# Filter spectra finished in the convolution's rounds instead of stored and reloaded, with smaller array tiles in the filters' first and the convolution's last stage

## The chip, the cores and the metric

The kernel runs on one core of a Trainium2 chip. The metric is the device time of one execution in microseconds, as a median of several runs. TensorE multiplies matrices, VectorE (DVE), ScalarE (ACT) and GpSimd (POOL) work on vectors, SyncE (SP) issues most of the DMA transfers.

## The reference

One layer of an encoder on a sequence of 2048 positions and 1024 channels, in float32. Half of the mixed channels go through a long convolution (the "Hyena" group), half through a two-directional mLSTM; cross-attention into 256 memory tokens and a squared-ReLU MLP follow. The part that the change touches is this:

```python
hid = jnp.sin(fr1 * (z @ w1 + b1))          # z: position features, 2048 x 33
hid = jnp.sin(fr2 * (hid @ w2 + b2))
filt = (hid @ w3).reshape(L, 2, 2, 512)     # order, direction, channel
filt = filt * jnp.exp(-t * jnp.abs(deltas))[:, None, None, :]
two_sided = jnp.concatenate([filt[:, :, 0], zeros, jnp.flip(filt[1:, :, 1], axis=0)])
spec = jnp.fft.rfft(two_sided, axis=0)      # 4096 points

z, g1, g2 = u[..., :512], u[..., 512:1024], u[..., 1024:]
for o, gate in enumerate((g1, g2)):
    conv = irfft(rfft(z, n=2 * L, axis=1) * spec[:, o], n=2 * L, axis=1)[:, :L]
    z = gate * (conv + z * skip[o])
```

So two filters (orders 0 and 1) are made, brought to the frequency domain, and the sequence is convolved with the one, gated, convolved with the other and gated again.

## The kernel before

**Products.** The large projections are done with each operand split into a high and a low part, three products for one (`mm3`, L361 to L363, called R products or sweep products below). The transforms use plain float32 products; each of these leaves two matmul records in the trace.

**The transform.** The 4096-point transform is done in two stages as matrix products. The position is split into a slow part (row q, 128 of them) and a fast part j (16 of them). The first stage multiplies by the constant `f1` along the rows, for each j and 512 channels. Its output is stored to DRAM in an order by (frequency, j), and read back so that the second stage can multiply by one of 32 constant matrices `dm` along (frequency part, j). Going back, `em` undoes the second stage and `e2` the first.

**The filters** (`filters`). After two sine layers, eight steps (j2) make, for both orders and two values of j each, the forward and the backward filter (`beside`, L177 and L185, two products on halves of the rows at once), window them, and form sum and difference e[0], e[1]. `front` multiplies each by a 128x128 half of `f1` (L297, one full product each), copies the result (L298) and stores it to `fs0`, `fs1`. Then `blocks` reads them back, and 32 steps (2 orders x 16) multiply by `dm` (L344, two products a step), copy on ScalarE (L345) and store the finished spectrum to `hd` (L346).

**The convolution** (`hyena`). First, `spectrum(0, ...)` for eight j2: loads z from `hy` (L823), two row pairs (L177, L185), copies (L903), stores to `zs` (L906). Then, for each order o: 16 rounds, in each of which `load2` has fetched `dm`, `em`, the block of `zs` (L856) and the real and imaginary part of the filter from `hd` (L858, L859), `double` copies these to the other half of the partitions (L863 on ScalarE, L867 on VectorE), two products with `dm` (L926), the complex multiplication on ScalarE (L928, L929), VectorE (L930, L932) and GpSimd (L931), and, one step later (`late`), the product with `em` (`back`, L892), a copy (L893) and a store to `zg`. Then eight steps go back to time: order 0 with column pairs (`beside` with 64 columns each, L177 and L185) and, a step later, `spectrum(1, ...)`, the joined stage; order 1 with four full products a step (L949), the gate (L950), and the group norm that writes `yh`.

**What sets the order.** `weave` interleaves two generators by the costs that they yield: `filters` with the first eight column sweeps of the input projection (weights 230 and 200), then `hyena` with the remaining sweeps and the `natural` products (227 and 382). Within this, a list scheduler orders the instructions of each engine when the program is built, and each engine, and SP's DMA queue, works through its list in order. `beside` gives its first product a priority and makes the second wait for readers of two earlier banks, so that all are released together. PSUM has eight banks: four with tag `mm` for the projections and four with tag `hy` for the transforms. The convolution's large tiles share one ring of 10 buffers (tag `a`).

Of the kernel before, what the change touches and what calls it, by code (L numbers as in the profile page):

```python
# [18 lines left out]
L = 2048  # L19
# [8 lines left out]
def shape_constants():  # L28
# [15 lines left out]
    c_win = np.stack([win, winb], 0)  # L44
# [17 lines left out]
    f1h = np.zeros((2, 2, 32, 2, 64))  # L62
    e2h = np.zeros((2, 2, 2, 64, 128))
    for h in range(4):
        f1h[h // 2, h % 2, :, h % 2] = own
        e2h[0, h // 2, h % 2, :, 32 * h:32 * h + 32] = inv
        e2h[1, h // 2, h % 2, :, h::4] = inv
# [9 lines left out]
    for par in range(2):  # L77
# [12 lines left out]
    dm = dm.reshape(32, 128, 128)  # L90
# [7 lines left out]
        "c_f1": f1.transpose(1, 0, 2),  # L98
        "c_f1h": f1h.reshape(128, 128),
        "c_e2h": e2h.reshape(4, 128, 128).transpose(1, 0, 2),  # L100
# [34 lines left out]
class Prog:  # L135
# [37 lines left out]
    def beside(self, first, second):  # L173
        n = self.banks.index(first[0].tensor.name)
        n = self.banks.index(first[0].tensor.name)
        held = self.banks[max(0, n - 4):max(0, n - 2)] if first[0].tensor.name != second[0].tensor.name else []
        b = self.nc.tensor.matmul(*second, start=True, stop=True)  # L177
# [6 lines left out]
        with self.tc.high_priority(2000):  # L184
            self.tc.keep_in_program_order(self.nc.tensor.matmul(*first, start=True, stop=True))  # L185
# [45 lines left out]
    def filters(self):  # L231
        nc, tc, a = self.nc, self.tc, self.a
        sd = [self.dram(f"fs{o}", (2, 128, 16, CH)) for o in range(2)]
        hd = self.dram("hd", (2, 32, 128, CH))
        sb, ta, tb = self.fsb, self.ta, self.tb
        if True:
# [4 lines left out]
            f1 = sb.tile([128, 2, 128], F32, name="f1")  # L241
            nc.scalar.dma_start(out=f1, in_=a["c_f1"])

            def sine(dst, src, b, fr, first=False):
# [11 lines left out]
                nc.scalar.activation(dst, u if len(dst.shape) == 2 else u.rearrange("p (q j) -> p q j", j=16), AF.Sin)  # L256

            hid = sb.tile([128, 16, 128], F32, name="hid")
            for c in range(4):
# [10 lines left out]
                sine(hid[:, :, 32 * c:32 * c + 32].rearrange("p j q -> p q j"), p2, 2, 3)  # L270
# [23 lines left out]
            def front(e, st, jj, o, js):  # L294
                for p in range(2):
                    pp = self.hy()
                    nc.tensor.matmul(pp, f1[:, p], e[p], start=True, stop=True)  # L297
                    nc.scalar.copy(st[p][:, jj], pp)  # L298
                    if jj == 1:
                        nc.sync.dma_start(out=sd[o][p, :, js], in_=st[p])  # L300

            nxt = windows(0)
            for j2 in range(8):
                js = slice(2 * j2, 2 * j2 + 2)
                yield 14
# [17 lines left out]
            def blocks(o, i):  # L323
                p, k = divmod(2 * i, 16)
                dm = sb.tile([128, 2, 128], F32, tag="dm", name="dm", bufs=3)
                d = nc.sync.dma_start(out=dm, in_=a["c_dm"][:, 2 * i:2 * i + 2])
                if o == 0 and i < 3:
                    tc.keep_in_program_order(d)
                t = ta()
                nc.sync.dma_start(out=t, in_=sd[o][p, 8 * k:8 * k + 16].rearrange("(k r) j c -> (r j) k c", k=2))  # L330
                return dm, t

            order = [(o, i) for o in range(2) for i in range(16)]
            q = [blocks(*order[0]), blocks(*order[1])]
            for n, (o, i) in enumerate(order):
                if True:
                    yield 3.4
                    dm, t = q.pop(0)
                    if n + 2 < 32:
                        q.append(blocks(*order[n + 2]))  # L340
                    hs = ta()
                    for m in range(2):
                        pp = self.hy()
                        nc.tensor.matmul(pp, dm[:, m], t[:, m], start=True, stop=True)  # L344
                        nc.scalar.copy(hs[:, m], pp)  # L345
                    nc.sync.dma_start(out=hd[o, 2 * i:2 * i + 2].rearrange("k l c -> l k c"), in_=hs)  # L346
# [1571 lines left out]
```

## Time and profile before

| | |
|---|---|
| median of 3 runs | 3288.78 us (3285.28, 3288.78, 3291.98) |
| profiled execution | 3292.63 us, span from first to last instruction 3290.9 us |
| busy, of the span | PE 94%, DVE 60%, ACT 46%, POOL 38% |
| mean granted TensorE clock | 0.975 |
| DMA | 655.75 MB, mean 199 GB/s |

The trace names a line, an engine, an operation and its tiles (out<-in). "x" is a count. Matmul records overlap their neighbours, since products are pipelined; the distance of their starts is what a product takes of TensorE. PEld is the loading of the fixed operand. The stretches of time in the prediction are us from the first instruction.

### The profile page before, as it was taken

To read this page: it belongs to the slowest core of one execution; us is meant where nothing else is said; L and a number is where in the kernel's file an instruction comes from. 1 tells how busy PE (TensorE), PEld (TensorE's weight loads), DVE (VectorE), ACT (ScalarE), POOL (GpSimd) and SP (SyncE) were. 2 spreads that over 40 slices of the span, in tenths; PEclk is the share of its full clock that TensorE was granted. 3 is DMA by queue.
4 is the path that set the end of the run, shared out by engine and by line. 5 is a ranking of instruction groups with operands and counts; after the bars stand their busy time and mean duration, and the time that the engine had idled before them with its cause. 6 is when DMAs were issued, how large, how long until landed. Compare 5 with 4: busy or idle time off the path is not lost.

```text
span 3290.9 us, 45063 instructions
## 1 busy us (share of the span) xinstructions
PE 3097.7 (94%) x15113; PEld 2470.2 (75%) x15113; DVE 1971.7 (60%) x3316; ACT 1502.7 (46%) x2842; POOL 1242.2 (38%) x863
## 2 busy tenths in 40 slices
PE   7999999898999996799999998999999999999998
PEld 5656665674667885698988896888788887888876
DVE  7765224535556664676766556665755686565695
ACT  5533445643663343444444435545555543333335
POOL 0122000210222214534433106886756574434483
PEclk9999999999999997899999999999999999999999
DMA  5554998888787679758465526664644475444434
GB/s 188 187 201 148 313 307 257 261 240 249 215 246 231 200 250 309 210 164 262 140 223 196 195 78 225 207 219 160 218 156 157 157 234 166 132 140 140 130 96 163
DMA packets 473903, 655.75 MB, mean 199 GB/s; under 512 B 41278, under 2 KB 253374, under 8 KB 472648
## 3 DMA queue, kind: packets, MB, share of 16 engines
q1 hardware_dynamic: 437796, 594.30, 58.0%
q10 hardware_dynamic: 35876, 58.57, 5.2%
q8 instruction: 120, 1.97, 0.3%
q14 instruction: 111, 0.91, 0.1%
HBM read 437.73 MB, written 214.99 MB: 198 GB/s over the span
## 4 chain that ended last, share of the span: by engine, by line
PE 66%; DMA 14%; DVE 8%; issue 5%; ACT 3%; POOL 2%; SPq 1%; ACTq 0%; DVEq 0%; POOLq 0%
PE mm L361 14%; PE mm L363 13%; PE mm L362 13%; PE hy L363 5%; PE hy L361 5%; PE hy L362 5%; DVE wl L366 2%; PE hy L344 2%; DMA rw<-rows 2%; PE hy L297 2%; DMA wn<-in_w_in_dram 1%; DMA a<-zg 1%; DMA a<-hd 1%; PE hy L177 1%; PE hy L892 1%
## 5 line engine op out<-in xcount | busy, mean ns | idle before, releaser
L366 DVE TENSOR_TENSOR wl<-wn,wh 128x512 fp32r<-128x512 f32 (+1 forms) x364 | 285.9, 820 | 147.8 <-ACT wh L366 144.0
L1499 DVE TENSOR_TENSOR bl<-wr,bh 128x512 fp32r<-128x512 f32 x213 | 239.0, 1129 | 125.2 <-ACT bh L1498 125.1
L1498 ACT CAST ah<-w 128x512 fp32r<-128x512 f32 x284 | 176.5, 623 | 301.2 <-PE hy L362 153.4
L366 ACT CAST wh<-wn 128x512 fp32r<-128x512 f32 (+1 forms) x364 | 209.3, 619 | 211.6 <-DMA wn<-in_w_in_dram 57.9
L931 POOL TENSOR_TENSOR b<-b,a 128x512 f32<-128x512 f32 x64 | 88.6, 1384 | 574.4 <-ACT b L929 406.2
L361 PE MATMUL mm<-xh,wh 128*128 128x512 f32 x640 | 278.0, 436 | 12.3 <-ACT xh L366 5.5
L362 PE MATMUL mm<-xl,wh 128*128 128x512 f32 x640 | 270.2, 423 | 2.2 <-DVE xl L366 1.6
L363 PE MATMUL mm<-xh,wl 128*128 128x512 f32 x640 | 263.2, 411 | 0.0
L1499 DVE TENSOR_TENSOR al<-w,ah 128x512 fp32r<-128x512 f32 x236 | 226.0, 959 | 61.4 <-ACT ah L1498 61.1
L1498 ACT CAST bh<-wr 128x512 fp32r<-128x512 f32 x232 | 143.9, 622 | 231.9 <-PE mm L363 173.9
L363 PE MATMUL mm<-bh,al 128*128 128x512 f32 x576 | 225.4, 394 | 7.6 <-DVE al L1499 4.4
L361 PE MATMUL mm<-bh,ah 128*128 128x512 f32 x576 | 227.0, 394 | 0.9 <-DVE u L1624 0.8
L362 PE MATMUL mm<-bl,ah 128*128 128x512 f32 x576 | 226.1, 393 | 0.0
L361 PE MATMUL mm<-act,wh 128*128 128x512 f32 x512 | 200.4, 395 | 2.9 <-ACT wh L366 2.9
L362 PE MATMUL mm<-act,wh 128*128 128x512 f32 x512 | 200.8, 392 | 0.0
L363 PE MATMUL mm<-act,wl 128*128 128x512 f32 x512 | 199.6, 393 | 0.1
L1355 POOL TENSOR_TENSOR ssum<-ssum,sq 128x512 f32<-128x512 f32 x56 | 80.3, 1433 | 274.5 <-ACT sq L1354 274.5
L361 PEld LDWEIGHTS mm<-xh,wh 128*128 128x128 f32 x640 | 123.0, 192 | 71.8 <-issue 29.9
L361 PE MATMUL hy<-bh,ah 128*128 128x512 f32 x448 | 175.2, 391 | 0.0
L362 PE MATMUL hy<-bl,ah 128*128 128x512 f32 x448 | 174.6, 390 | 0.0
L363 PE MATMUL hy<-bh,al 128*128 128x512 f32 x448 | 174.4, 390 | 0.0
L362 PEld LDWEIGHTS mm<-xl,wh 128*128 128x128 f32 x640 | 122.7, 192 | 53.8 <-issue 26.2
(368 smaller groups left out, 8785.5 us busy)
## 6 DMA issues: line engine op xcount, KB each, us to landing
wr<-hc SPq DMA_DIRECT2D x224, 256.0 KB
w<-in_ff_w_dram SPq DMA_DIRECT2D x176, 256.0 KB
hc<-t SPq DMA_DIRECT2D x128, 256.0 KB
wn<-in_w_in_dram SPq DMA_DIRECT2D x100, 256.0 KB
hc<-q SPq DMA_DIRECT2D x96, 256.0 KB
fs<-a SPq DMA_DIRECT2D x32, 512.0 KB
a<-fs SPq DMA_DIRECT2D x32, 512.0 KB
hd<-a SPq DMA_DIRECT2D x32, 512.0 KB
```

The lines of the kernel that those rows point to most:

```text
L177: b = self.nc.tensor.matmul(*second, start=True, stop=True)
L297: nc.tensor.matmul(pp, f1[:, p], e[p], start=True, stop=True)
L344: nc.tensor.matmul(pp, dm[:, m], t[:, m], start=True, stop=True)
L361: mm(ps, lh, rh, start=start, stop=False)
L362: mm(ps, lh, rl, start=False, stop=False)
L363: mm(ps, ll, rh, start=False, stop=stop)
L366: both = (self.nc.scalar.copy(hi, src), self.nc.vector.tensor_tensor(lo, src, hi.bitcast(F32), ALU.subtract))
L892: nc.tensor.matmul(pg, em[:, m], y, start=True, stop=True)
L931: nc.gpsimd.tensor_tensor(xt, xt, hi[:, m], ALU.mult)
L1355: nc.gpsimd.tensor_tensor(ssum, ssum, sq, ALU.add)
L1498: self.nc.scalar.copy(hi, src)
L1499: eng.tensor_tensor(lo, src, hi.bitcast(F32), ALU.subtract)
```

## The change

- `filters` ends after `front`. The second stage (`blocks`, its 32 steps, the tensor `hd`) is gone.
- `hyena` loads the filter's first-stage output itself (`load_filter`: `dm` and two halves of a block of `fs`), two rounds ahead, and `response` makes the filter's spectrum one round ahead: two products with `dm` into `mm` banks, each evacuated by four copies of 64 partitions, two on ScalarE, two on VectorE. `double` is gone.
- `front` uses four products of 64 rows by 64 columns, for e[0], e[1] and two groups of 64 rows each, through a `beside` that takes any number of products. Each of its two banks receives one quarter from each row group.
- Rows are ordered as two groups of 64 by parity of q. With it, order 1's last stage becomes column pairs like order 0's, and constants and DMA patterns change: z, gates and `yh` move as two DMAs of 64 partitions, `zs` stores and `zg` loads as one of 128 partitions, `zs` loads and `zg` stores as two of 64.
- The yielded costs and the two weights of `weave` change.

```diff
-    def beside(self, first, second):
-        n = self.banks.index(first[0].tensor.name)
-        n = self.banks.index(first[0].tensor.name)
-        held = self.banks[max(0, n - 4):max(0, n - 2)] if first[0].tensor.name != second[0].tensor.name else []
-        b = self.nc.tensor.matmul(*second, start=True, stop=True)
+    def beside(self, *products):
+        names = [p[0].tensor.name for p in products]
+        n = min(self.banks.index(t) for t in names)
+        held = self.banks[max(0, n - 4):max(0, n - 2)] if len(set(names)) > 1 else []
+        b = self.nc.tensor.matmul(*products[-1], start=True, stop=True)
...
-            self.tc.keep_in_program_order(self.nc.tensor.matmul(*first, start=True, stop=True))
+            for p in reversed(products[:-1]):
+                self.tc.keep_in_program_order(self.nc.tensor.matmul(*p, start=True, stop=True))
...
             def front(e, st, jj, o, js):
+                pp = [self.hy() for p in range(2)]
+                self.beside(*((pp[p][64 * (p ^ g):64 * (p ^ g) + 64], f1[64 * g:64 * g + 64, 64 * p:64 * p + 64],
+                               e[p][64 * g:64 * g + 64]) for p in range(2) for g in range(2)))
                 for p in range(2):
-                    pp = self.hy()
-                    nc.tensor.matmul(pp, f1[:, p], e[p], start=True, stop=True)
-                    nc.scalar.copy(st[p][:, jj], pp)
+                    nc.scalar.copy(st[p][:, jj], pp[p])
...
-                yield 14
+                yield 9
...
-            def blocks(o, i):
-                p, k = divmod(2 * i, 16)
-                dm = sb.tile([128, 2, 128], F32, tag="dm", name="dm", bufs=3)
-                d = nc.sync.dma_start(out=dm, in_=a["c_dm"][:, 2 * i:2 * i + 2])
...
-                    for m in range(2):
-                        pp = self.hy()
-                        nc.tensor.matmul(pp, dm[:, m], t[:, m], start=True, stop=True)
-                        nc.scalar.copy(hs[:, m], pp)
-                    nc.sync.dma_start(out=hd[o, 2 * i:2 * i + 2].rearrange("k l c -> l k c"), in_=hs)
...
+        def load_filter(o, i):
+            dm = sb.tile([128, 2, 128], F32, tag="dm", name="dm", bufs=3)
+            nc.sync.dma_start(out=dm, in_=a["c_dm"][:, 2 * i:2 * i + 2])
+            p, k = divmod(2 * i, 16)
+            t = ta()
+            for g in range(2):
+                nc.sync.dma_start(out=t[own[g]], in_=of_block(fs[o][p, 64 * (p ^ g):64 * (p ^ g) + 64], k))
+            return dm, t
...
-            nc.sync.dma_start(out=hr[0:64], in_=src[0])
-            nc.sync.dma_start(out=hi[64:128], in_=src[1])
-            return dm, em, t, hr, hi
-
-        def double(i, hr, hi):
-            nc.scalar.copy(hr[64:128], hr[0:64])
...
-            nc.vector.tensor_copy(hi[0:64], hi[64:128])
+        def response(i, dm, t):
+            hr, hi = ta(), ta()
+            for m in range(2):
+                pp = self.mm()
+                nc.tensor.matmul(pp, dm[:, m], t[:, m], start=True, stop=True)
+                nc.scalar.copy(hr[0:64, m], pp[0:64])
+                nc.scalar.copy(hr[64:128, m], pp[0:64])
+                nc.vector.tensor_copy(hi[64:128, m], pp[64:128])
+                nc.vector.tensor_copy(hi[0:64, m], pp[64:128])
...
+            fq = [load_filter(o, i) for i in range(2)]
             nxt = load2(o, 0)
+            ready = response(0, *fq.pop(0))
             for i in range(16):
-                yield 3.5
-                dm, em, t, hr, hi = nxt
+                yield 4.6
+                dm, hr, hi = ready
+                em, t = nxt
+                if i < 14:
+                    fq.append(load_filter(o, i + 2))
                 if i < 15:
                     nxt = load2(o, i + 1)
+                    ready = response(i + 1, *fq.pop(0))
...
-                    if o == 0:
-                        own = [slice(64 * b, 64 * b + 64) for b in range(2)]
-                        self.beside(*((pp[own[b]], e2[:, b, own[b]], r[b][:, jj]) for b in range(2)))
-                    else:
-                        for p in range(2):
-                            nc.tensor.matmul(pp, e2[:, 2 + p], r[p][:, jj], start=p == 0, stop=p == 1)
+                    self.beside(*((pp[own[g]], e2, r[g][:, jj]) for g in range(2)))
...
-            weave(p.filters(), s, 230, 200)
+            weave(p.filters(), s, 80, 200)
...
-                      227, 382)
+                      271, 382)
```

118 lines of the change are left out of this document (47 added, 71 removed).

## The prediction

> **What bounds the kernel now.** I read the page first, then a table of time stretches, then the timeline at three places to get the true price of a matrix product, then the groups of the operations that the diff removes or adds, the DMA issues and the chain.
>
> ```profile
> PE 3097.7 (94%) x15113; PEld 2470.2 (75%) x15113; DVE 1971.7 (60%) x3316; ACT 1502.7 (46%) x2842; POOL 1242.2 (38%) x863
> DMA  5554998888787679758465526664644475444434
> ```
>
> TensorE is busy 94% of the span, VectorE 60%. The DMA digits say that slices 4 to 14 (330 to 1230 us) run their DMA engines at 70% or more. That is where the changed stages lie, so the stretches come next: filters' front (100 to 350), filters' second stage (350 to 480, the part that goes), and the convolution: first spectrum, rounds of order 0, the joined stage (order 0 back to time and spectrum of order 1), rounds of order 1, last stage.
>
> ```profile
> core 0: us, PE busy (x) PEld busy (x) DVE busy (x) ACT busy (x) POOL busy (x), PEclk, DMA share, GB/s
> 100.00:350.00 250.00, 240.66 (x920) 150.47 (x920) 158.72 (x254) 97.86 (x157) 56.24 (x32) 0.97 0.54 180
> 350.00:480.00 130.00, 130.00 (x473) 86.06 (x472) 26.41 (x40) 62.50 (x101) 0.00 (x0) 1.00 0.94 321
> 480.00:548.00 68.00, 62.96 (x254) 39.38 (x253) 26.66 (x39) 24.54 (x38) 0.00 (x0) 1.00 0.89 253
> 548.00:700.00 152.00, 138.41 (x727) 101.37 (x725) 76.63 (x122) 98.47 (x161) 41.97 (x32) 1.00 0.86 257
> 700.00:812.00 112.00, 96.52 (x487) 61.23 (x486) 46.32 (x70) 27.45 (x49) 0.00 (x0) 0.94 0.90 249
> 812.00:1004.00 192.00, 182.74 (x691) 127.11 (x689) 111.80 (x159) 123.74 (x187) 46.60 (x32) 0.96 0.76 221
> 1004.00:1130.00 126.00, 119.76 (x787) 101.47 (x786) 86.69 (x192) 38.52 (x77) 35.38 (x22) 0.97 0.81 247
> ```
>
> Between 350 and 480 us TensorE has no idle time at all, although DMA stands at 0.94 and 321 GB/s: that stage is bound by TensorE's work, and its traffic runs beside it. In the convolution TensorE idles 5.0, 13.6, 15.5, 9.3 and 6.2 us of the five stretches, lower bounds, because a record lasts beyond the start of the next. So the stretch from 100 to 1130 us is TensorE work plus some 50 us of stalls, and the change is worth what it takes from either. Bytes and copies are worth something only where they end a stall.
>
> A product's mean duration is no price, since products overlap. The pitch is.
>
> ```profile
> 392.19 0.39 PE L362 MATMUL mm<-xl,wh 128*128 128x512 f32 x1
> 392.42 1.02 PE L344 MATMUL hy<-a,dm 128*128 128x512 f32 x2
> 392.88 0.80 PE L363 MATMUL mm<-xh,wl 128*128 128x512 f32 x1
> 393.52 0.40 PE L361 MATMUL mm<-xh,wh 128*128 128x512 f32 x1
> ...
> 510.03 0.39 PE L361 MATMUL mm<-xh,wh 128*128 128x512 f32 x1
> 510.25 0.39 PE L362 MATMUL mm<-xl,wh 128*128 128x512 f32 x1
> 510.57 0.69 PE L177 MATMUL hy<-a,f 64*128 64x512 f32 x1
> ...
> 511.63 0.50 PE L363 MATMUL mm<-xh,wl 128*128 128x512 f32 x1
> 511.97 0.39 PE L361 MATMUL mm<-xh,wh 128*128 128x512 f32 x1
> ...
> 711.01 0.28 PE L362 MATMUL mm<-wl,xh 128*128 128x256 f32 x1
> 711.13 0.28 PE L363 MATMUL mm<-wh,xl 128*128 128x256 f32 x1
> 711.34 0.64 PE L177 MATMUL hy<-a,e 128*64 128x512 f32 x1
> 711.34 0.64 PE L185 MATMUL hy<-a,e 128*64 128x512 f32 x1
> ...
> 713.20 0.39 PE L361 MATMUL mm<-wh,xh 128*128 128x256 f32 x1
> 713.42 0.28 PE L362 MATMUL mm<-wl,xh 128*128 128x256 f32 x1
> ```
>
> First part: from 392.19 to 393.52 there are one full float32 product (two records) and two sweep products of 0.23 us pitch (510.03 to 510.25 shows the pitch): 1.33 - 0.46 = **0.87 us for a full product**. Second: from 510.25 to 511.97 one row pair (two products on halves of the rows) and two sweep products: 1.72 - 0.46 = **1.26 us for a lone row pair**, that is 0.87 for both halves at once and 0.39 for entering and leaving the split array. Third: from 711.13 to 713.42 two column pairs and two sweep products at 0.12: **2.05 us for two column pairs**, which is 2 x 0.87 and 0.3. L177 and L185 start at the same moment there, though both stream through all rows: column halves run side by side.
>
> The Trainium skill, "TensorE: Matmul & The Clock Gate", section "Measured speedup vs the span model", has a packed group last one product and about 4 ns for each further tile. By it the 32 groups of four below would cost 28 us and the front would give 27. The row of the lone pair shows 0.39 us more than one product, so I don't go by it.
>
> **The change part by part.**
>
> ```profile
> L297 PE MATMUL hy<-b,f 128*128 128x512 f32 x128 | 65.5, 624 | 0.0
> L949 PE MATMUL hy<-a,e 128*128 128x512 f32 x64 | 30.8, 624 | 2.8 <-DMA a<-zg 2.8
> L345 ACT COPY a<-hy 128x512 f32<-128x512 f32 x64 | 37.5, 587 | 62.1 <-PE hy L344 62.0
> L863 ACT COPY a<-a 64x1024 f32<-64x1024 f32 x32 | 33.5, 1046 | 73.6 <-DMA a<-hd 73.5
> L867 DVE COPY a<-a 64x1024 f32<-64x1024 f32 x32 | 22.1, 690 | 58.0 <-DMA a<-hd 50.0 <-DMA em<-in_c_em_dram 3.6 <-DMA kn<-st 2.8
> L903 DVE COPY a<-hy 128x512 f32<-128x512 f32 x32 | 21.6, 687 | 15.2 <-PE hy L185 9.8 <-DMA a<-hy 5.2
> L928 ACT ACTIVATE b<-hy 64x512 f32<-64x512 f32 x64 | 38.2, 596 | 8.2 <-PE hy L926 3.6 <-ACT a L893 1.9 <-DVE b L930 0.6
> ```
>
> *Filters' front on quarters.* 128 records of L297 are 64 full products: 64 x 0.87 = 55.7 us. They become 32 groups of four 64x64 products. No row shows four at once; row halves and column halves each do. Ends: 0.87 for a group (all four together) and 3.48 (one after another). I take 0.87 and 0.39 for the switch, because both kinds of pair behave so. In the changed program's order three of the 32 groups are parted by sweep products, so 35 passes: 35 x 1.26 = 44.1. **Saved: 11.6 us** (28 if switches cost nothing).
>
> *Last stage in column pairs.* 64 records of L949 are 32 full products, 27.8 us; now 8 times two column pairs, 8 x 2.05 = 16.4. **Saved: 11.4 us.** The third row block above is the operation itself, so this is the safest term.
>
> *Second filter stage, moved into the rounds.* L345 has 64 copies, one for each product: 64 x 0.87 = 55.7 us of TensorE work that stays, and moves from a stretch without idle time into the rounds. **0** on TensorE. Copies: ScalarE loses 37.5 + 33.5 and gains 128 half copies of 0.596 (L928's form), 76.3: +5 us in all, but +43 inside the rounds. VectorE loses 22.1 and gains 128 copies at 0.687 (L903 reads the same 512 columns of a bank), 87.9: +66 us, 2.1 us in each of 32 rounds. In the order-1 rounds VectorE would go from 111.8 of 192 us to about 145 of 220, 66%; ScalarE likewise to 66%. Neither becomes the bound; both queues get longer. The response of round i+1 stands ahead of round i's own products, so its copies have a round to finish, and they are queued ahead of the multiplications of L930 and L932 that `back` waits for.
>
> *DMA.* What goes is the store of hd and its two reloads, and the second read of dm.
>
> ```profile
> hd<-a SPq DMA_DIRECT2D x32, 512.0 KB
> a<-hd SPq DMA_DIRECT2D x64, 256.0 KB
> dm<-in_c_dm_dram SPq DMA_DIRECT2D x64, 128.0 KB
> a<-hy SPq DMA_DIRECT2D x64, 128.0 KB
> zs<-a SPq DMA_DIRECT2D x32, 256.0 KB
> zs<-a ACTq DMA_DIRECT2D x32, 256.0 KB
> ```
>
> That is 16.8 + 16.8 + 4.2 = 38 MB less; the reads of fs stay and take hd's place in a round, so a round's traffic is as now, while its TensorE work grows from four to six full products. DMA eases, most of it where it hid anyway.
>
> *What this does to the stalls.* Here the changed program's order decides. (a) Joined stage, now 15.5 us idle at a clock of 0.94 and DMA 0.90: in the new order 75 to 100 sweep products of 0.12 us stand between column pairs, 9 to 12 us, against 33 to 55 now. More cover for the same loads: -10 (ends -15 and 0). (b) Rounds, 13.6 + 9.3 idle now: counting products between L926's and its L892's place, the cover grows from 6 to 9 us to 7.5 to 12; against it stand the longer VectorE and ScalarE queues: -5 (ends -15 and +20, the latter if 0.6 us a round is waited for). (c) First spectrum stage, 5.0 idle now: its row pairs stand 17 sweep products apart today; in the new order 14 of the 16 stand back to back, with nothing between, and 24 sweep products follow after two responses before the first round. On SP's queue stand, each behind the other, z's loads, half of the stores to zs and the sweep's next weights. The pairs need 16 x 0.87 = 14 us. Until the last pair all eight loads must land (4.2 MB) and about four of the eight double stores (4.2 MB, since ten buffers hold 3.3 rounds), three loads earlier than the first pair: 6.8 MB at 0.29 MB/us between the rows' 253 and 321 GB/s is 24 us. So 10 us of idle time and some 3 at the handover, instead of 5: +8 (ends -5 and +36, below).
>
> Sum: -11.6 - 11.4 - 10 - 5 + 8 = **-30 us**. The profiled execution took 3292.63 us (span 3290.9), 3.9 above the median of 3288.78 and beside the slowest of the three runs; taken from the median, the forecast is **3259 us**, -0.9%.
>
> **The rivals.**
>
> *The first stage waits on its transfers (slower).* The same mechanism as (c) at its full price: all loads and stores of the stage, 12.6 MB, go through before TensorE proceeds, at 253 GB/s 50 us, with the landing of the last store behind it and the next load behind that.
>
> ```profile
> 498.21 4.84 DMA zs<-a
> ...
> 544.86 5.36 DMA a<-hd
> ```
>
> The second row stands for the load of the first block. 50 - 14 + 10 - 7 (two responses and 24 sweep products as cover) is 39 of idle time, +34. Where the transfers set the pace, (a) and (b) give nothing: -23 + 34 = +11, 3300 us. It decides from about 30 us of idle time in that stage on. For it: DMA at 0.89 in this stretch even when the pairs are spread, and stores among the longest steps of the chain. Against: half of the stores go out on ScalarE's queue, and nothing but the last rounds' buffers makes a load wait for a store.
>
> *The four quarters do not run together.* Two quarters on different rows write the same bank, on different partitions, and no row of the trace shows that; all row pairs here write two banks. If they take turns, a group costs 1.74 + 0.39: 32 x 2.13 = 68 against 55.7, +12 instead of -11.6, 3283 us. The Trainium skill, "TensorEngine Tiling (Array Packing)", section "Gotcha 1: PSUM Pressure", says that different row tiles cannot access one PSUM bank at the same time, which would give this. The column pairs, which share a bank across partitions and start together at 711.34, speak for the opposite.
>
> *The rounds' queues eat it.* (b) at its upper end: +25 against my sum, 3284 us. For it: 66% on two engines, with VectorE's L867 already behind DMA waits. Against: more cover in every round.
>
> *More is gained.* The lower ends of (a), (b), (c) with -23: 3231 us.
>
> **How the numbers follow.** Forecast 0.52; more gained 0.15; quarters in turn 0.08; queues 0.05; first stage 0.20. Of these the first two are faster by over 0.2% (6.6 us, about what a measurement of this kernel can tell), 0.67; the quarters and the queues lie at -5 to -6 us, within 0.2%, 0.13; the first stage is slower, 0.20. The forecast's own range is 3240 to 3277. The range to hold 8 in 10 runs from the upper part of "more gained", 3234, to just short of the full first stage, 3297.
>
> **What would show it.** In the new profile: quarter products starting within 0.2 us of each other in fours, next sweep product about 1.3 us later (else the second rival); last-stage column pairs at 2.05 us for two; the stretch from 100 us to the end of the last stage about 30 us shorter; the first spectrum stage with 10 to 15 us idle, the joined stage with 5; DMA bytes down by 38 MB. I am wrong if the first stage idles over 30 us, or if the rounds show TensorE waiting for L930's and L932's successors or for the copies of the response.

## The result and the profile after

| | before | after |
|---|---|---|
| median, us | 3288.79 (3285.28 to 3291.98, 4 runs) | 3241.74 (3236.51 to 3245.18, 4 runs) |
| ratio, 95% interval | 1 | 0.9854 [0.9836, 0.9872] |
| profiled execution; span, us | 3292.63; 3290.9 | 3245.18; 3243.5 |

The kernel became 47 us faster; 30 had been forecast. On the page of the profile after, TensorE's busy share is unchanged, VectorE has the extra copies, and the DMA moved 38 MB less than the 655.75 MB of before.

```profile
PE 3061.6 (94%) x15241; PEld 2442.3 (75%) x15241; DVE 2029.8 (63%) x3414; ACT 1499.1 (46%) x2871; POOL 1246.7 (38%) x863
PEclk9999899999999998999999999999999999999999
DMA packets 451633, 617.72 MB, mean 190 GB/s; under 512 B 39614, under 2 KB 247614, under 8 KB 450376
```

The table of stretches, cut at the new stage limits (front; first spectrum; rounds of order 0; joined; rounds of order 1; last stage), has the columns of the one in the prediction: time, its length, busy time of PE, PEld, DVE, ACT and POOL, granted clock, DMA share, GB/s.

```profile
100.00:371.00 271.00, 266.71 (x1244) 165.16 (x1242) 169.28 (x273) 107.39 (x177) 57.37 (x32) 1.00 0.54 172
371.00:421.00 50.00, 33.56 (x102) 15.27 (x102) 19.91 (x31) 15.96 (x28) 0.00 (x0) 0.76 0.99 316
421.00:624.00 203.00, 196.72 (x794) 134.31 (x794) 125.21 (x193) 135.80 (x225) 44.39 (x32) 0.98 0.73 203
624.00:753.00 129.00, 116.41 (x731) 85.68 (x731) 45.40 (x71) 32.71 (x64) 0.00 (x0) 0.93 0.77 242
753.00:964.00 211.00, 203.99 (x750) 135.87 (x750) 145.90 (x208) 140.71 (x228) 46.23 (x32) 1.00 0.72 197
964.00:1096.00 132.00, 118.95 (x799) 99.91 (x799) 93.38 (x206) 41.26 (x78) 42.04 (x28) 0.95 0.77 222
```

The second row is the new weak place: in the first spectrum stage 16 of 50 us are idle by records (the length of the stretch less TensorE's busy time), the DMA engines are full (0.99) and the granted clock is 0.76. The rounds (third and fifth row) are dense, with VectorE at 62% and 69%, and DMA at 0.73 and 0.72 where it stood at 0.86 and 0.76.

Busy time overstates work, since records overlap and grow longer at a low clock. So I also count each stage's *work* by pitch: number of products times 0.227 us (sweep, 512 columns), 0.120 (256 columns), 0.109 (transposition), 0.858 (full float32 product, or a pair or four of them side by side; full products back to back start at 421.55, 422.41, 423.27 and 424.12 us). What is left of the stage's length I call *idle*: waits, switches of the array and time lost to a low clock together. The front is counted from 100 us on; the stages run from the first product of one kind to the first of the next, the last one to the mLSTM's first transposition ("end"). "Filler" counts the narrow products (256 columns) ahead of that point. The other kernels of this table come below.

| length (idle), us | before | after | both_full | filler_back | before_filler | spread_first | spread_cover |
|---|---|---|---|---|---|---|---|
| front | 251.5 (29.3) | 271.1 (35.3) | 280.5 (19.1) | 270.2 (35.8) | 250.6 (29.3) | 269.5 (35.1) | 269.0 (35.5) |
| filters' second stage | 131.1 (2.1) | none | none | none | 131.3 (2.3) | none | none |
| first spectrum | 65.2 (11.2) | 50.4 (27.3) | 48.8 (23.9) | 50.5 (20.2) | 64.6 (10.6) | 65.7 (8.1) | 69.1 (6.1) |
| rounds, order 0 | 163.6 (17.0) | 202.4 (10.6) | 197.2 (6.4) | 218.9 (6.6) | 164.9 (18.3) | 202.8 (9.5) | 199.1 (11.3) |
| joined | 111.8 (34.5) | 129.5 (24.7) | 129.4 (24.5) | 124.0 (18.4) | 125.1 (25.4) | 109.9 (22.9) | 114.4 (16.9) |
| rounds, order 1 | 191.5 (19.1) | 210.5 (9.5) | 207.4 (6.4) | 220.9 (6.8) | 189.4 (16.5) | 197.4 (2.9) | 192.7 (9.1) |
| last | 126.3 (8.5) | 132.2 (23.8) | 135.8 (18.6) | 109.2 (14.1) | 128.7 (11.2) | 126.4 (25.0) | 120.7 (19.7) |
| end, us | 1140.9 | 1096.1 | 1099.0 | 1093.7 | 1154.5 | 1071.5 | 1065.1 |
| time behind the end | 2149.9 | 2147.4 | 2152.5 | 2145.0 | 2145.0 | 2154.6 | 2150.8 |
| filler | 1173 | 1051 | 1010 | 1288 | 1362 | 1089 | 1084 |

Of the 47.4 us that the span lost, 44.8 lie ahead of "end". The work ahead of it fell by 54.5 us: 27.5 for the front's quarters (64 to 32 passes of 0.858), 13.7 for the column pairs (32 to 16), and 14.6 because 122 filler products now come later, less 1.4 for six more sweep products. The idle time grew by 9.5; switches of the array, by the two prices that follow, add at most 16 to it (35 x 0.37 and 8 x 0.34), so the waits and the low clock fell by up to 6.

The timeline around a group of four in the front:

```profile
146.54 0.39 PE L337 MATMUL mm<-xl,wh 128*128 128x512 f32 x1
146.86 0.64 PE L175 MATMUL hy<-b,f 64*64 64x512 f32 x1
146.87 0.65 PE L184 MATMUL hy<-b,f 64*64 64x512 f32 x3
147.34 0.59 PE L175 MATMUL hy<-b,f 64*64 64x512 f32 x1
147.35 0.60 PE L184 MATMUL hy<-b,f 64*64 64x512 f32 x3
147.88 0.50 PE L338 MATMUL mm<-xh,wl 128*128 128x512 f32 x1
148.22 0.39 PE L336 MATMUL mm<-xh,wh 128*128 128x512 f32 x1
```

The four quarters start within 0.01 us of each other, twice (each product leaves two records). From 146.54 to 148.22 stand the group and two sweep products: 1.68 - 0.45 = 1.23 us for four quarters, 0.37 above one pass. In the last stage:

```profile
1003.74 0.29 PE L337 MATMUL mm<-wl,xh 128*128 128x272 f32 x1
1003.95 0.64 PE L175 MATMUL hy<-a,e 128*64 128x512 f32 x1
1003.96 0.64 PE L184 MATMUL hy<-a,e 128*64 128x512 f32 x1
...
1005.30 0.59 PE L184 MATMUL hy<-a,e 128*64 128x512 f32 x1
1005.82 0.39 PE L338 MATMUL mm<-wh,xl 128*128 128x272 f32 x1
1006.05 0.29 PE L336 MATMUL mm<-wh,xh 128*128 128x272 f32 x1
```

From 1003.74 to 1006.05 stand two column pairs and two products of 272 columns (0.127 us each): 2.31 - 0.25 = 2.06 us. Both prices are those of the prediction.

From the first spectrum stage and its handover to the rounds:

```profile
384.20 0.62 ACT L341 CAST wh<-wn 128x512 fp32r<-128x512 f32 x1 [4.49 <-DMA wn<-in_w_in_dram]
...
385.35 1.22 PE L175 MATMUL hy<-a,f 64*128 64x512 f32 x1 [4.07 <-ACT a L883]
...
398.28 0.66 PE L175 MATMUL hy<-a,f 64*128 64x512 f32 x1 [3.20 <-DMA a<-hy]
...
398.79 0.59 PE L175 MATMUL hy<-a,f 64*128 64x512 f32 x1
...
402.67 1.06 PE L175 MATMUL hy<-a,f 64*128 64x512 f32 x1
...
403.52 1.06 PE L175 MATMUL hy<-a,f 64*128 64x512 f32 x1
...
410.56 3.75 PE L840 MATMUL mm<-a,dm 128*128 128x512 f32 x4 [5.09 <-DMA a<-fs]
413.32 1.42 PE L336 MATMUL mm<-xh,wh 128*128 128x512 f32 x1
414.53 0.63 PE L337 MATMUL mm<-xl,wh 128*128 128x512 f32 x1
414.96 0.63 PE L338 MATMUL mm<-xh,wl 128*128 128x512 f32 x1
```

The pairs wait twice for ScalarE's copies (L883; 2.6 and 4.1 us; ahead of the second ScalarE itself had waited 4.5 us for the sweep's next weights), later for z's loads (3.2 us), and then the first response (L840) waits for the filter's load, which stands behind z's loads and the stores on SP's queue. Between the waits the products themselves are slow: the distance of two records is 0.85 us at 402.67 and 0.51 at 398.28, and the sweep products at 414.53 come every 0.43 us instead of 0.23.

The waits that fell on TensorE between 345 and 1150 us, the four largest of after (instruction, releaser, us in total, times, longest):

```profile
PE mm L840 <- DMA a<-fs: 17.9, 3, 9.0
PE hy L175 <- ACT a L883: 8.4, 3, 4.1
PE hy L175 <- DMA a<-zg: 5.4, 2, 4.0
PE mm L739 <- DVE cv L706: 3.9, 1, 3.9
```

and the largest of before in the same stretch:

```profile
PE hy L892 <- DVE b L932: 9.5, 9, 2.3
```

Before, the largest was `back` waiting, nine times, in the middle of the rounds for the complex multiplication. After, that wait is no longer among the large ones. Two of the three waits for a<-fs are at the handovers, for an order's first filter block (5.1 us at 410.56 and 9.0 at 743.17); the third, 3.8 us at 581.09, is inside order 0's rounds. The other rows are single waits in the first spectrum, joined and last stage.

### The profile page after: what moved, and what is told of

Read it like the earlier page. It is cut to its first block, busy times and chain, and to the rows that moved or that the text cites. A ratio compares the mean times of both kernels' runs of the same rounds, so it can differ in the third digit from the quotient of the medians.

```text
span 3243.5 us, 45260 instructions
## 1 busy us (share of the span) xinstructions
PE 3061.6 (94%) x15241; PEld 2442.3 (75%) x15241; DVE 2029.8 (63%) x3414; ACT 1499.1 (46%) x2871; POOL 1246.7 (38%) x863
## 4 chain that ended last, share of the span: by engine, by line
PE 74%; DMA 12%; DVE 7%; issue 3%; ACT 2%; POOL 1%; SPq 1%; ACTq 0%; DVEq 0%; POOLq 0%
PE mm L336 16%; PE mm L337 15%; PE mm L338 15%; PE hy L338 5%; PE hy L336 5%; PE hy L337 5%; PE hy L175 3%; PE mm L840 2%; PE hy L910 2%; PE hy L871 2%; DVE wl L341 1%; DVE bl L1479 1%; DMA wn<-in_w_out_dram 1%; DMA wn<-in_xa_wo_dram 1%; DMA rw<-rows 1%
## 5 line engine op out<-in xcount | busy, mean ns | idle before, releaser
L341 ACT CAST wh<-wn 128x512 fp32r<-128x512 f32 (+1 forms) x364 | 208.4, 617 | 196.3 <-PE mm L337 50.5
L337 PE MATMUL mm<-xl,wh 128*128 128x512 f32 x640 | 260.2, 407 | 2.2 <-DVE xl L341 1.6
L319 POOL TENSOR_TENSOR b<-b 128x512 f32<-128x512 f32 x32 | 57.4, 1793 | 295.4 <-DVE b L314 133.6
```

The source lines that it names most:

```text
L337: mm(ps, lh, rl, start=False, stop=False)
L341: both = (self.nc.scalar.copy(hi, src), self.nc.vector.tensor_tensor(lo, src, hi.bitcast(F32), ALU.subtract))
```

## The experiments

The question was which part carried the gain, and why the moved second stage might be worth more than the -7 us that the prediction's stall terms gave it (-10 - 5 + 8). Ratios are to the kernel before on the same chip, five rounds each, with 95% intervals. Listings are cut to the edit.

**The parts undone one by one.** *front_full*: the changed kernel with full products in the front.

```diff
-                pp = [self.hy() for p in range(2)]
-                self.beside(*((pp[p][64 * (p ^ g):64 * (p ^ g) + 64], f1[64 * g:64 * g + 64, 64 * p:64 * p + 64],
-                               e[p][64 * g:64 * g + 64]) for p in range(2) for g in range(2)))
...
+                    nc.tensor.matmul(pp, f1w[:, p], e[p], start=True, stop=True)
```

> The changed kernel with the filters' front on two full products again (the quarters put into a 128x128 constant with zeros elsewhere). Theory (product pitch): 64 full products at 0.87 us against 32 groups of four at 1.23 us in the new trace, so about +16 us, 3258 us, all of it between 100 us and the first spectrum pair. Rival (the front is paced by VectorE and GpSimd, not by TensorE): no change, 3242 us. Rival (the front's end moves, but the first spectrum stage, which waits for its transfers, takes the loss up): +5 us or less.

Measured: 3252.62 us, 0.9883 [0.9863, 0.9904], so about +9.5 us against the changed kernel (the two intervals overlap), between the expected 16 and the rivals. Its front lasted 279.8 us instead of 271.1: 27.5 us of work came back, 11 sweep products fewer stand there, and idle time, the switches of the array among it, fell from 35.3 to 19.0.

*last_full*: the changed kernel with two full products a value of j in order 1's last stage.

```diff
-                    self.beside(*((pp[own[g]], e2, r[g][:, jj]) for g in range(2)))
...
+                        for g in range(2):
+                            nc.tensor.matmul(pp, e2w[:, g], r[g][:, jj], start=g == 0, stop=g == 1)
```

> The changed kernel with order 1's last stage on four full products a step again (two accumulated, the constant filled up with zeros). Theory (product pitch): 32 full products at 0.87 against 8 times 2.05 us, +11 us, 3253 us. Rival: the last stage idles in the new trace for transfers and for VectorE (gaps of 4.2, 4.1 and 2.4 us), so the longer products fill gaps: +4 us or less.

Measured: 3246.31 us, 0.986 [0.984, 0.9881]: +2 us against the changed kernel, not to be told from nothing. 13.7 us of work came back, idle time in that stage fell from 23.8 to 16.4, and the convolution ended at 1090.8, 5 us *earlier* than with column pairs (41 filler products fewer, 4.9 us, stand ahead of its end).

*both_full*: both edits, so that only the moved second stage (with the row order, the yielded costs and the weights) is left of the change.

> Both of the above: what is left of the change is the filters' second stage moved into the rounds, with its DMA traffic gone. If the terms add, +27 us, 3269 us, and moving the stage alone is worth 20 us against the kernel before. If the whole gain came from the smaller array tiles, 3289 us. If the moved stage carries nearly all of it, under 3255 us.

Measured: 3256.18 us, 0.989 [0.987, 0.991]. Undoing both costs 12 us and not 27; what is left, the moved stage in its new order, is worth 36 us. Its rounds:

```profile
429.30:626.50 197.20, 192.37 (x784) 131.64 (x782) 123.76 (x192) 133.50 (x221) 44.38 (x32) 1.00 0.74 207
755.90:963.30 207.40, 203.23 (x748) 135.78 (x746) 145.17 (x207) 140.31 (x227) 45.85 (x32) 1.00 0.72 196
```

TensorE stands idle 4.8 and 4.2 us in them by its records, where before it was 13.6 and 9.3. With the table: idle time of rounds and joined stage falls from 17.0 + 34.5 + 19.1 = 70.6 to 6.4 + 24.5 + 6.4 = 37.3. That is 33.3 us of gain, and it is not the whole account. The front's idle time fell by 10.2 as well (716 sweep products stand in it for 551; granted clock 1.00 for 0.97); the first spectrum stage (with the second stage's 2.1 before) and the last stage idle 10.6 and 10.1 us more; and 163 filler products (19.6 us) slid behind the convolution, where the time grew by 2.6. Together the convolution ends 41.9 us earlier. Is it the bytes, the copies, or the TensorE work inside the rounds that ends the waits, and did the sliding of the filler matter?

**The bytes.** *more_traffic*: the changed kernel, and every round also stores its finished spectrum to a spare tensor that nobody reads.

```diff
+            nc.sync.dma_start(out=spare[0, i], in_=hr)
+            nc.sync.dma_start(out=spare[1, i], in_=hi)
```

> The changed kernel with the removed DMA traffic put back without its use: each round also stores hr and hi (512 KB each) to a scratch tensor, 33.5 MB in all, as much as the store of hd and its reloads were. Theory A (the moved stage gains because TensorE finds more of its own work between a round's products, bytes do not matter): within 5 us of the changed kernel, 0.9854 +- 0.002 of the kernel before. Theory B (the rounds stalled less because DMA was relieved by 38 MB): most of the 35 us that the moved stage is worth goes, ratio 0.993 or more.

Measured: 3239.53 us, 0.9841 [0.9821, 0.986], no slower than without. The DMA moved 651.29 MB. So the bytes saved are not the cause of the gain.

**Work in the rounds, without the change.** *idle_products*: the kernel before with two more products with `dm` in each round, whose output is not read.

```diff
+                    nc.tensor.matmul(self.mm(), dm[:, m], t[:, m], start=True, stop=True)
+                for m in range(2):
```

> The kernel before with two more full products in each round of the convolution, on the round's own dm and t into an mm bank that nobody reads: 64 products, 55.7 us of TensorE work by the pitch, and no change of DMA, copies or stages. Their result is not used. Theory A (cover): they fill stalls of the rounds (17.0 and 19.1 us idle there now, 10.6 and 9.5 in the changed kernel), and some 15 to 20 us of the sweep products move behind the convolution's end, where the mLSTM's first part leaves TensorE idle; so about +20 us, ratio 1.006. Theory B (DMA relief, TensorE is the bound): +50 us or more, ratio 1.015 or more.

Measured: 3348.8 us, 1.0188 [1.0174, 1.0202], far above Theory A's 1.006 and within Theory B's bracket (1.015 or more). The rounds by themselves did as Theory A has it: their idle time fell from 36.1 to 18.1 us with no byte and no copy less. But the interleaving changed ahead of them: the row pairs of the first spectrum stage came to stand back to back there too, and the handovers opened.

```profile
474.00:525.00 51.00, 27.38 (x69) 10.96 (x70) 11.07 (x16) 10.44 (x18) 0.00 (x0) 0.67 0.93 275
```

```profile
PE mm L925 <- DMA a<-zs: 21.2, 2, 10.8
PE hy L177 <- DMA a<-hy: 12.7, 2, 10.8
```

So this run mixed two things. *order1_products* puts the products into order 1's rounds alone (`for m in range(2 * o)`), which leaves the order of the stages ahead of them as it was.

> The kernel before, with two more products with dm in each of order 1's rounds and nothing else; their outputs are not read, so the result is the same. It puts the moved stage's TensorE work (16 x 2 x 0.87 = 27.9 us) into one set of rounds without touching the order of the stages ahead of them, which the version with products in both orders did. No bytes go. 159 of the narrow filler products slide behind the convolution (19.1 us), as there. Theory A (a round's own chain of loads, copies and multiplications sets its pace, and TensorE work that stands in it fills the wait): TensorE's idle time in order 1's rounds falls from 19.1 us to 6 to 8, the convolution ends at 1140.9 + 27.9 - 12 - 19 = 1138 us, and the whole takes 0 to +10 us against the kernel before, ratio 1.000 to 1.003. Rival (the idle time goes only because fewer bytes and no copies from hd are waited for): idle time stays at 17 to 19 us, the end at 1150 us, the whole +10 to +20, ratio 1.003 to 1.006.

Measured: 3311.31 us, 1.0061 [1.0043, 1.0079].

```profile
824.00:1022.00 198.00, 193.87 (x700) 127.24 (x698) 102.36 (x148) 115.41 (x175) 42.98 (x32) 0.99 0.68 197
```

```profile
PE mm L925 <- DMA a<-zs: 11.1, 1, 11.1
```

The idle time in order 1's rounds fell from 19.1 to 7.6 us, as Theory A said: they took 6.1 us longer (197.6 against 191.5) for 27.9 us of added work, of which 11.5 filled waits and some 10 stand in the place of filler or ahead of the rounds. The total went with the rival, for other reasons than the rival's: the filler that had covered the handover slid away and a wait of 11.1 us opened there (joined stage, idle 34.5 to 44.3), and the time behind the convolution grew by 11.8 us. Both theories missed those two.

**More cover by order alone.** *later_back*: the kernel before with `back` run two steps later instead of one, with two more `b` buffers and one more for `em`.

```diff
-                    late(lambda m=m, em=em, y=y, gs=gs, dst=by_block(gd, i): back(m, em, y, gs, dst))
+                    late(lambda m=m, em=em, y=y, gs=gs, dst=by_block(gd, i): back(m, em, y, gs, dst), 2)
```

> The kernel before with `back` (the product with em) two steps behind its round's product instead of one, and buffers for it (b 7, em 3). It adds cover between the two products, 1 to 1.5 us in the order built from it, and takes no work and no bytes away. Theory A (rounds stall on the chain from dm's product to em's): 10 to 20 us faster, ratio 0.995. Theory B: no change, ratio 1.000 +- 0.002.

Measured: 3273.4 us, 0.9958 [0.9945, 0.997]. The total came out at Theory A's size, but not by its mechanism: idle time in the rounds was 22.9 + 17.7 = 40.6 us and did not fall. But 41 us of other TensorE work, 21.6 of it filler, left the rounds in this order, so it is no clean test of cover; the waits of `back` for L932 still came to 8.0 us (9.5 before). The joined stage's idle time fell from 34.5 to 22.4, and 19 us of filler slid behind the end, where the time grew by 7.

**The filler.** It slid in nearly every kernel that was faster, so it could have been the gain. *filler_back*: the changed kernel with one weight of `weave` lowered.

```diff
-                      271, 382)
+                      240, 382)
```

> The changed kernel with one weight of the interleaving, 240 for 271, so that 1288 instead of 1051 of the narrow filler products stand before the mLSTM's first transposition: 237 x 0.12 = 28.4 us of TensorE work back into the convolution. Theory A (work behind the convolution is nearly free, since the mLSTM's first part leaves TensorE idle; so what counts is when the convolution ends): the convolution ends 15 to 28 us later, by what of the work does not fill a wait (30 sweep products now stand among the first row pairs too, and take 3 to 7 us of idle time there), the time behind it shortens by no more than 5 us, and the whole takes +12 to +22 us against the changed kernel, ratio to the kernel before 0.989 to 0.992. Rival (total TensorE work sets the time, wherever it stands): the time behind the convolution shortens by as much as the convolution grows, whole 0 to -7 us against the changed kernel, ratio 0.983 to 0.9855.

Measured: 3242.02 us, 0.9852 [0.9835, 0.987]. 28.4 us of TensorE work put back cost nothing, and the convolution still ended at 1093.7 us. Theory A's bracket (+12 to +22) is wrong. The rival's total fits, but not its mechanism: the time behind the end shrank by only 2.4 us. The work went into idle time: 131.2 us in all before, 101.9 now. Three stretches of it (first spectrum, joined, last):

```profile
370.00:421.00 51.00, 38.35 (x143) 20.19 (x142) 21.61 (x35) 18.22 (x32) 0.00 (x0) 0.87 0.97 320
640.00:764.00 124.00, 115.88 (x633) 80.25 (x630) 59.46 (x91) 39.87 (x69) 0.00 (x0) 0.97 0.84 265
985.00:1094.00 109.00, 100.83 (x746) 86.49 (x742) 78.39 (x181) 33.07 (x70) 39.64 (x28) 1.00 0.90 262
```

The granted clock is 0.87, 0.97 and 1.00 where the changed kernel had 0.76, 0.93 and 0.95. Length times missing clock gives at most 12 + 9 + 7 = 28 us lost there after, and 7 + 4 + 0 = 11 here: by these bounds up to 17 of the 29 us of idle time that went may be clock that was kept up.

*before_filler*: the same done to the kernel before (210 for 227).

> The kernel before with one weight of the interleaving, 210 for 227: 1362 instead of 1173 narrow filler products stand ahead of the mLSTM's first transposition, 189 x 0.12 = 22.7 us of TensorE work into the convolution. In the changed kernel 28.4 us of the same filler cost nothing (ratio 0.9852 against 0.9854; the convolution even ended 2.4 us earlier), because its stages wait for their own loads, stores and copies. Theory A (the same holds before the change: the convolution's own chain sets its end, and filler falls into waits): the convolution ends 0 to 6 us later, the whole -4 to +4 us, ratio 0.999 to 1.001. Rival (before the change TensorE's work counts, and the change made it stop counting by moving the second filter stage into the rounds): the convolution ends 15 to 23 us later, the time behind it shortens by 2 to 8 us, the whole +10 to +18 us, ratio 1.003 to 1.0055.

Measured: 3304.45 us, 1.0048 [1.0035, 1.0062], as the rival had it. The end came 13.6 us later (the rival said 15 to 23) for 22.7 us of work; the joined stage took all of it, and gave 9 us of idle time for it:

```profile
711.00:836.00 125.00, 112.56 (x537) 74.61 (x536) 60.12 (x91) 36.65 (x61) 0.00 (x0) 0.97 0.88 241
```

So in the kernel before, added TensorE work shows up in the time, and in the changed kernel it doesn't, as these two weights place it. The sliding of 122 products is not what the changed kernel gained by: with 115 more of them than the kernel before had, it is as fast.

**The handovers.** *spread_first*: the changed kernel with twice the yield in the first spectrum stage, so that sweep products stand between its row pairs again.

```diff
-            yield 4
+            yield 8
...
-                      271, 382)
+                      303, 382)
```

> The changed kernel with the first spectrum stage yielding 8 instead of 4 a step (and 303 for 271 in the weights), which in the order built from it puts sweep products between the row pairs again, where the changed kernel has 14 of 16 pairs back to back. Nothing else is changed. Theory: the stage from 371 to 413 us of the new trace idles some 25 us for transfers and runs its products at a lower clock after it; spread, 15 to 20 us of that go, 3222 to 3227 us. Rival: the stage is bound by its loads and stores, and the sweep products put in front only shift where TensorE waits later: 3242 us.

Measured: 3227.53 us, 0.9803 [0.9783, 0.9823], at the upper end of the expected range (3222 to 3227) and faster than the changed kernel.

```profile
369.00:435.00 66.00, 63.63 (x263) 40.02 (x261) 30.76 (x48) 30.91 (x48) 0.00 (x0) 1.00 0.87 279
```

```profile
PE mm L840 <- DMA a<-fs: 5.6, 1, 5.6
```

The first spectrum stage is at full clock with 2 us without a record, and the waits for a<-fs fell from 17.9 to 5.6 us. *spread_early* also issues the first two filter loads of order 1 earlier, from within the joined stage; order 0's stay where they were.

```diff
+                    if j2 == 6:
+                        early = [load_filter(1, i) for i in range(2)]
```

> spread_first, with the first two filter blocks of an order loaded earlier (for order 0 ahead of the spectrum stage's end, for order 1 in the joined stage's seventh step), so that the first response does not wait for them (9.5 us at the joined stage's end in the changed kernel). Theory: part of that wait goes, the rest is the round trip of zs that the first round waits for anyway: 3 to 8 us faster than spread_first, ratio 0.979. Rival: the round trip of zs sets the handover: no change, 0.980.

Measured: 3226.9 us, 0.9817 [0.9803, 0.983], no gain, as the rival had it. The wait only changed its name: the products of the first round now wait for the round trip of zs.

```profile
PE hy L912 <- DMA a<-zs: 10.8, 2, 9.0
```

*spread_cover* therefore puts work there instead of moving the load: a further yield ahead of each order's first response.

```diff
+            yield 10
             ready = response(0, *fq.pop(0))
...
-                      303, 382)
+                      323, 382)
```

> The version with the spread first stage and one further yield of 10 ahead of the first response of each order (with the weight of the interleaving raised from 303 to 323), so that more filler stands at both handovers into the rounds: 16.3 us before order 0's rounds and 10.6 us before order 1's, against 5.4 each. Theory A (the waits left at the handovers are the round trip of the stores to zs and their reload, and work that stands there covers it): the waits at both handovers shrink by 4 to 8 us each, the convolution ends 5 to 12 us earlier than in the spread version, ratio to the kernel before 0.977 to 0.9795. Rival (the filler is only moved there from another place, which then waits): 0.979 to 0.982, no difference from the spread version at 0.9803.

Measured: 3219.93 us, 0.9783 [0.9762, 0.9803]; the end came 6.4 us earlier than in the spread version, at 1065.1, in Theory A's range. The intervals of the two overlap, so this last step is likely, not certain; against both the kernel before and the changed kernel (0.9854) the version is clearly faster. The waits at the two handovers are gone: in the spread version they were 2.5 us for a<-zs ahead of order 0's rounds and 5.6 us for a<-fs ahead of order 1's, here none is above 0.2 us. The first response of order 1, first in the spread version, then here:

```profile
736.06 3.75 PE L840 MATMUL mm<-a,dm 128*128 128x512 f32 x4 [5.57 <-DMA a<-fs]
```

```profile
743.93 1.99 PE L840 MATMUL mm<-a,dm 128*128 128x512 f32 x4 [0.17 <-ACT P L685]
```

So Theory A's mechanism held, with waits of 2.5 and 5.6 us to gain for its 4 to 8 each. The joined stage's idle time fell from 22.9 to 16.9 us and the last stage's by 5, but other waits opened inside the rounds (the largest 3.25 us for a<-fs at 533.64), which idle 8 us more.

## Why the prediction was right, and where not

The sign and the range held. The result lies at the lower end of the forecast's own range (3240 to 3277), 17 us short of the likeliest value. That it is no more than 17 is partly luck: the moved stage was put at -7 and gave 36 us, 29 more, and the two tile edits were put at -23 and gave 12, 11 less.

*Front on quarters, -11.6.* The price was right (1.23 for 1.26). Undoing it cost 9.5 us by the ratios, whose intervals overlap, and 8.6 by the front's length. Right in size.

*The quarters take turns.* Excluded by the rows at 146.86. The bank rule of the Trainium skill, "TensorEngine Tiling (Array Packing)", section "Gotcha 1: PSUM Pressure", does not hold for writes to different partitions of one bank here: the group cost 1.23 us, not 2.13. By an estimate from the span model of the Trainium skill, "TensorE: Matmul & The Clock Gate", section "Measured speedup vs the span model", four tiles would cost 12 ns more than one. Here the group cost 0.37 us more, with entering and leaving the split array.

*Column pairs, -11.4.* The price was right to 0.01 us, and the term was called the safest; it is worth 2 us, not told from none. The failing step is adding it to the sum as time. The last stage's idle time went from 8.5 to 23.8 us, a term that the prediction did not have at all; when the products were put back, idle time fell by 7.4 us. By records it went from 4.4 to 13.1 us, and 6.3 of that are three waits of the projections' products for VectorE (3.9, 1.4 and 1.0 us, at 994.84, 1003.50 and 1012.86), where a column sweep ends: its last 48 products stand in this stage after, and none before.

*(a) Joined stage, -10.* By records, the prediction's measure, 15.5 us idle became 12.6 and not 5; by the table 34.5 became 24.7, since the records had hidden much of what there was. So the fall is about the 10 us that were forecast, but from a higher level. The cover works: *before_filler*, which put 22 us of work into this stage of the kernel before, brought its idle time to 25.4. 9.0 us of the rest is one wait for a<-fs ahead of the first response of order 1, which was not foreseen. That load is issued at 734.00 us, behind a store to zs and the sweep's loads on SP's queue, and takes 8.1 us:

```profile
743.17 3.75 PE L840 MATMUL mm<-a,dm 128*128 128x512 f32 x4 [8.99 <-DMA a<-fs]
```

*(b) Rounds, -5.* By records 22.9 became 13.3, by the table 36.1 became 20.1: -10 to -16, towards the lower bound (-15). The step that failed is weighing the longer VectorE and ScalarE queues against the cover: they cost nothing that shows. *order1_products* shows the mechanism alone: with 27.9 us of products added, order 1's rounds lose 11.5 us of idle time. The same seen from the side of the work: "0 on TensorE" for the moved stage was mis-sized, since its 55.7 us left a stretch with 2 us of idle time and went to one with 36, where some 18 us of them (*idle_products*, both orders) were free.

*(c) First spectrum stage, +8.* By records 5.0 became 16.4, by the table 13.3 (with the second stage's 2.1) became 27.3: +11 to +14. The bunching and the queueing were foreseen. Not priced was the clock: 0.76 over 50 us is up to 12 us. The first rival had the right mechanism, waiting for transfers, but its 39 us idle were 16.4 by records and 27.3 by the table, low clock and switches included.

*DMA hidden.* Right: 33.6 MB more in *more_traffic* changed nothing.

*The front's stalls* were put at nothing: "some 50 us" leaves out the 9.3 us that the first row of the prediction's table shows idle between 100 and 350 us. By records they fell to 4.3 us. A smaller slip is that not all of slices 4 to 14 have their DMA engines at 70% or more: slice 13, from 1070 us, is a 6. No term rests on that.

*The rounds' queues eat it.* False: the wait for L932's successor (L916) is no longer among the large ones, though VectorE is busy 69% of order 1's rounds.

The deeper fault was the form of the sum: TensorE work plus stalls, each term standing by itself. The terms belong together. Alone, the moved stage gave 36 us, the two tile edits gave 12 on top of it instead of 23, since afterwards TensorE work is no longer what these stages are short of: 28.4 us more of it cost nothing after, while 22.7 us more cost 14 to 16 before.

Left open: why nothing covers the sweep's end in the last stage (other kernels with 48 sweep products there idle 8 to 10 us in it); why the time behind the end lies anywhere from 2145 to 2162 us (it was longest in the kernels that pushed most filler there, but not in strict order); and how much of the 36 us comes from the new order as such, the 163 filler products among it that the kernel with only the moved stage pushed back, since the filler was put back only in the fully changed kernel.

## What to carry to other kernels

Work moved from a stage without idle time to one that waits for its own chain is partly free; price it by the idle time at its new place and not by its duration. Once stages wait for their own loads and copies, cheaper matrix products there buy little, and cheap independent work put between the dependent products buys more: it ends waits and keeps the clock up (spreading eight row-pair steps was worth 17 us here by the ratios, 0.9803 for 0.9854). When a kernel's order is made by weights, look where the filler went before a difference is put down to an edit.

## What was not expected of the hardware

Four 64x64 products on all four quarters, two to a bank, run side by side: 1.23 us, against 0.87 for one full product and 1.26 for a pair on two row halves.

After waits of a few us TensorE runs at half speed for a while: row pairs at 0.85 us per record instead of 0.43 to 0.51, sweep products at 0.43 instead of 0.23. In the first spectrum stage the granted clock was 0.50 from 378.9 to 389.0, from 399.4 to 406.1 and from 409.6 to 416.4 us, about the waits of 2.59, 4.07, 3.20 and 5.09 us. The last of these stretches:

```profile
409.60:416.40 6.80, 5.84 (x10) 3.33 (x11) 2.37 (x4) 2.89 (x5) 0.00 (x0) 0.50 0.69 242
```

The Trainium skill, "TensorE: Matmul & The Clock Gate", Part 1, has the clock halved after an idle window of about 3.4 us and whole again after as long a busy one. The return agrees roughly: it came 3.7 us after the products set in again at 385.35 and 5.8 us after 410.56. The waits that halved it were in part shorter here, 2.59 and 3.20 us. In the stage's spread version, where no wait above 0.2 us stands between the pairs, the granted clock is 1.00.
